# RWKV-7 steps on one core: PSUM banks shared out anew, first tokens in another order, new places for every piece, 16 projection pieces in each of the last steps

## The chip, the cores and the metric

The kernel runs on one core of a Trainium2 chip. What counts is the device time of one launch in microseconds (us). The kernel before was timed three times: 2500.08, 2500.66 and 2507.4 us, median 2500.66 us.

## What is computed

A decoder trunk of two layers over 2048 tokens of width 1024, all in float32. Layer 1 mixes tokens with gated linear attention (GLA), layer 2 with RWKV-7. Each layer is `x <- x + RMSNorm_post(mixer(RMSNorm_pre(x)))`. The RWKV-7 mixer, cut to what matters here:

```python
p = h @ w_in                          # 4224 columns: r, k, v, gate, decay rank 64, iclr rank 64
p = p + mu * (token_shift(p) - p)
decay = exp(-exp(w_log));  a = sigmoid(a0 + ad @ w_iclr_up)
def step(S, inp):                     # one token, 16 heads, S is 64 x 64 a head
    r_t, w_t, k_t, v_t, kk_t, a_t = inp
    sa = einsum('bhvk,bhk->bhv', S, -kk_t)
    S = S * w_t[:, :, None, :] + sa[..., None] * (kk_t * a_t)[:, :, None, :] + v_t[..., None] * k_t[:, :, None, :]
    y = einsum('bhvk,bhk->bhv', S, r_t)
    return S, y
y = groupnorm(y) * ln_w + ln_b + bonus
y = y * silu(gate);  return y @ w_out
```

## The kernel before, in words

**Stages.** The GLA layer comes first, with its output projection to about 911 us. Then RWKV runs in 32 steps (4 blocks of 512 tokens times 8 pairs of heads), and after the steps the rest of the output projection (`outproj`). A matrix product in nearly full precision is three products of split operands: `mm3` (L114) multiplies the high parts, high by low, and low by high. The high and low part of a weight are made by `split`; in the RWKV stage POOL makes them at L990 (`wh<-ws`) and L994 (`wl<-ws,wh`) in part of the pieces.

**One step.** `step` (L1144) works on 8 chunks of 64 tokens for two heads. Its pieces on TensorE (PE) are named by functions: `pA` the decayed products of keys and receptances (four pieces; mask L1370 on VectorE (DVE) takes them out of PSUM), `pL`, `pM`, `pW`, `pT` small 32x32 products that build the inverse of a triangular matrix, `pB` transposes, `pv` the values (two pieces; ScalarE (ACT) copies them out at L1325, `ve`), `pX` the product with the inverse `Ti` (ACT L1544 copies it to `Z`), `turn` transposes (ACT L1568), `pG` products whose results DVE adds to `BK` and `A` at L1583 (`G`), `pS` the chain of 8 states (ACT L1604, `next_state`, the last one L1604 into `S`), `py` the outputs (ACT L1618, `y_copy`), and `pg` the group norm's sums, which needs `y_sq` (L1623), `y_high` (L1628) and `y_low` (DVE L1633) of the outputs of the step before.

**Filler.** Between those pieces stand `f` pieces: a sixteenth of the projection work that the next step needs, 6 matmuls 128x512 each (`ps_pj<-R,wh` and `ps_pj<-R,wl`), called a chunk below. A step has 16 of them (12 in one early step, 20 in each eighth step by `MORE`). After the last step `END` gives how many still run in each further step: 12, with every fourth name of the sixteen left out.

**The order of the work.** Around the change the order is written out by hand: `put` (L86) gives each piece the time step number + `PLACE[name]`, `run` (L95) calls the pieces in that order under a manual schedule of PE, DVE, ACT and POOL. So the table `PLACE` sets the order on all four queues at once. A piece of step n with a place of 2.05 runs during step n+2; a step's work is spread over three to four steps.

**PSUM.** Eight banks, by the table `PB` (L70): `pj` 2 (projections), `tp` 2 (most of the step), `x` 1, `ch` 2 (states `pS` and `pg`), `y` 1. A new tile of a tag waits until the reader of the tile that had its bank is done.

```python
PB = dict(pj=2, tp=2, x=1, ch=2, y=1)
T.pv = self.ps("tp", [P, NC_ // 2, 2, C])
T.pA[cg] = [self.ps("tp", [P, 4, 2 * C]) for _ in range(2)]
T.pG[cg] = [self.ps("tp", [P, 4, 2 * C]) for _ in range(2)]
T.pS[c] = self.ps("ch", [P, 2, C])
```

**The start.** `start` (L566) orders the first four blocks of 128 tokens by hand: `square(j)` (ACT L328, waits for the tokens' DMA), `scale(j)` (POOL L308, DVE L337), `turn(j, k)` (PE transposes L343, ACT copy L345), weight splits `W0`, `W1`, `W2` (ACT L163, POOL L164), and `values(n)`, n pieces of the values' projection.

Of the kernel before, what the change touches and what calls it, by code (L numbers as in the profile page):

```python
# [50 lines left out]
class Trunk:  # L51
# [1035 lines left out]
    END = (12, 12, 12, 12)
    PLACE = _places(
        ("G", (2.044193, 2.050266, 2.091647, 2.158500)), ("Ti", (1.943141, 1.843493, 1.792896, 1.843393)),
        ("Tl", (1.896995, 1.931904)), ("X", (1.565836, 1.565936, 1.799057, 1.860390)), ("Z", (2.011437, 2.021714)),  # L1090
        ("a_exp", 0.211357), ("a_inv", 0.235809), ("a_ln", 0.212886), ("ae", (0.264280, 0.264380)),
        ("alpha", (1.784826, 1.830405, 1.928084, 1.927784)), ("bk_b", (0.393193, 0.393293)), ("bk_copy", 0.491543),
        ("bk_k", 0.393093), ("bonus", 0.827316), ("diag", (0.630464, 0.666138, 0.714265, 0.692811)),
        ("e", (1.976686, 0.550686, 0.225756, 0.383364)), ("e_minus", 0.227189), ("e_plus", 0.301397),
        ("elim", (0.804391, 0.807537, 0.807637, 0.871330, 0.906435, 0.906535, 0.906635, 0.906735, 0.937961, 0.960696,
          1.011273, 1.015145, 1.034379, 1.077861, 1.100228, 1.103822, 1.103922, 1.104449, 1.104549, 1.127910,
          1.134421, 1.135126, 1.136468, 1.158139, 1.187233, 1.196122, 1.210237, 1.248533)),
        ("ends", 0.408256), ("eye", (1.693688, 1.735073, 1.968882, 1.940955)),
        ("f", (0.255319, 0.000000, 0.050514, 0.774971, 0.318264, 0.976958, 0.509575, 0.349895, 0.478398, 0.529148,
          0.559227, 0.085857, 0.815059, 0.191123, 0.714834, 1.258740)),  # L1100
# [606 lines left out]
```

## Time and profile before

| what | before |
|---|---|
| median of the runs | 2500.66 us |
| the profiled execution, its own time | 2500.48 us |
| its span, first to last instruction | 2498.4 us |
| PE busy | 2404.0 us (96%) |
| ACT busy | 1646.3 us (66%) |
| DVE busy | 1601.1 us (64%) |
| POOL busy | 1065.7 us (43%) |
| mean granted clock of TensorE | 0.991 |

The span is what the profile covers; 2.1 us of the execution lie around it. Busy shares are means over stages with different limits. PE is nearly always busy, so the time is PE's work plus the stretches in which PE waits, and a piece that only changes its place costs or saves what it does to those waits.

### The profile page before, as it was taken

The page shows a single profiled execution, that of the slowest core. Times are in us where ns is not written, and L with a number is a line of the kernel's source. Part 1 is how long each engine was busy: PE and PEld are TensorE (multiplying, and loading weights), DVE is VectorE, ACT ScalarE, POOL GpSimd, SP SyncE. Part 2 cuts the span into 40 slices and gives each one's busy share as a digit, 9 for nine tenths or more (in the row PEclk, how much of TensorE's full clock was granted, in tenths as well). Part 3 has the DMA queues.
Part 4 walks back from the last instruction along what each step waited for, and adds up shares of the span by engine and source line. Part 5 has one row for each costly group of instructions (what it writes and reads, how often), then busy time and mean ns, then how long its engine had stood idle before and what let it go on. Part 6 is the DMA issues. An engine that isn't in the chain of part 4 may idle for free.

```text
span 2498.4 us, 53047 instructions
## 1 busy us (share of the span) xinstructions
PE 2404.0 (96%) x20049; PEld 2011.4 (81%) x20049; DVE 1601.1 (64%) x3339; ACT 1646.3 (66%) x3890; POOL 1065.7 (43%) x1557
## 2 busy tenths in 40 slices
PE   7999999999999998989999999999999999998998
PEld 6988888898878877767878788778788777887777
DVE  6544676346743368887777776777767787776432
ACT  6534565434533356876888988888888889886531
POOL 3213423123456556766543434334343434343442
PEclk9999999999999999998999999999999999999999
DMA  4211333113546565444433333333333333323482
GB/s 148 81 57 51 110 114 104 43 60 95 165 149 223 162 221 176 145 141 138 150 113 132 125 118 114 109 120 125 124 110 114 113 123 123 120 88 111 149 256 93
DMA packets 251863, 312.85 MB, mean 125 GB/s; under 512 B 18746, under 2 KB 180185, under 8 KB 251609
## 3 DMA queue, kind: packets, MB, share of 16 engines
q1 hardware_dynamic: 251608, 309.47, 37.4%
q8 instruction: 159, 2.61, 0.4%
q14 instruction: 96, 0.78, 0.1%
HBM read 230.77 MB, written 78.64 MB: 124 GB/s over the span
## 4 chain that ended last, share of the span: by engine, by line
PE 37%; ACT 18%; DVE 4%; issue 2%; DMA 1%; POOL 1%; POOLq 0%; SPq 0%; ACTq 0%; DVEq 0%
PE ps_pj L103 20%; PE ps_tp L103 9%; PE ps_x L103 3%; ACT AD L1380 2%; PE ps_ch L103 2%; ACT ve L1604 2%; ACT ts L836 1%; ACT ve L1325 1%; PE ps_y L103 1%; ACT BK L1397 1%; ACT y L1618 1%; PE ps_tp L1564 1%; ACT wt L1495 1%; ACT sq L1278 1%; DVE pp L1422 1%
## 5 line engine op out<-in xcount | busy, mean ns | idle before, releaser
L103 PE MATMUL ps_pj<-R,wh 128*128 128x512 f32 x3648 | 1172.8, 402 | 3.8 <-ACT wh L139 1.0
L103 PEld LDWEIGHTS ps_pj<-R,wh 128*128 128x128 f32 x3648 | 656.5, 190 | 131.0 <-issue 3.4
L103 PE MATMUL ps_pj<-R,wl 128*128 128x512 f32 x1824 | 718.2, 394 | 1.1 <-POOL wl L994 1.1
L103 PEld LDWEIGHTS ps_pj<-R,wl 128*128 128x128 f32 x1824 | 343.8, 188 | 79.8 <-POOL wl L994 1.9
L1604 ACT ACTIVATE ve<-ps_ch,cs 64x64 f32<-64x64 f32 x448 | 137.8, 308 | 61.3 <-PE ps_ch L103 52.5
L1422 DVE TENSOR_TENSOR pp<-L 128x14 f32<-128x14 f32 (+6 forms) x448 | 168.1, 375 | 10.5
L103 PE MATMUL ps_tp<-R,wh 128*128 128x512 f32 x512 | 158.3, 390 | 2.1 <-DVE ts L400 1.7
L1425 DVE TENSOR_TENSOR L<-L,pp 128x14 f32<-128x14 f32 (+6 forms) x448 | 139.9, 312 | 12.2
L832 POOL TENSOR_SCALAR carr<-ts 128x1 f32<-128x1 f32 x132 | 34.2, 259 | 241.1 <-ACT ts L836 240.8
L1551 POOL TENSOR_SCALAR A<-ra 64x512 f32<-64x512 f32 x128 | 90.0, 703 | 103.4 <-PE ps_x L103 51.9
L308 POOL TENSOR_TENSOR s<-s,cc 128x1 f32<-128x1 f32 (+1 forms) x96 | 57.6, 602 | 150.7 <-DVE s L306 138.4
L103 PE MATMUL ps_ch<-ve,BK 128*128 128x128 f32 x512 | 109.5, 296 | 7.8 <-ACT ve L1604 7.5
L103 PEld LDWEIGHTS ps_tp<-R,wh 128*128 128x128 f32 x512 | 95.8, 188 | 22.8 <-issue 2.5
L103 PEld LDWEIGHTS ps_ch<-ve,BK 128*128 128x128 f32 x512 | 87.1, 189 | 30.9 <-ACT ve L1604 11.4
L1380 ACT COPY AD<-A 32x128 f32<-32x128 f32 x256 | 105.1, 411 | 10.2 <-DVE A L1370 7.2
L836 ACT ACTIVATE ts<-ps_pj,prm 128x512 f32<-128x512 f32 x132 | 91.4, 692 | 18.7 <-PE ps_pj L103 10.7
L1370 DVE TENSOR_TENSOR A<-ps_tp,mask 128x512 f32<-128x512 f32 x128 | 82.3, 683 | 32.6 <-PE ps_tp L103 32.6
L103 PE MATMUL ps_tp<-R,wl 128*128 128x512 f32 x256 | 99.7, 390 | 0.0
L1583 DVE TENSOR_TENSOR BK<-ps_tp,BK 128x256 f32<-128x256 f32 x128 | 53.7, 419 | 69.6 <-PE ps_tp L103 69.6
L103 PE MATMUL ps_pj<-wh,R 128*128 128x256 f32 (+1 forms) x500 | 94.7, 287 | 0.0
L103 PE MATMUL ps_ch<-wh,R 128*128 128x256 f32 (+1 forms) x500 | 94.3, 286 | 0.0
L798 POOL TENSOR_SCALAR y<-BK,cs 128x256 f32<-128x256 f32 x64 | 36.6, 571 | 132.4 <-DVE BK L800 121.3
(358 smaller groups left out, 5518.3 us busy)
## 6 DMA issues: line engine op xcount, KB each, us to landing
wh<-w SPq DMA_DIRECT2D x99, 512.0 KB
wl<-w SPq DMA_DIRECT2D x99, 512.0 KB
w<-wh SPq DMA_DIRECT2D x33, 512.0 KB
w<-wl SPq DMA_DIRECT2D x33, 512.0 KB
Ti<-in_gla_w_in_dram SPq DMA_DIRECT2D x32, 512.0 KB
ws<-in_gla_w_in_dram SPq DMA_DIRECT2D x32, 512.0 KB
ws<-in_rwkv_w_in_dram SPq DMA_DIRECT2D x28, 512.0 KB
A<-in_x_dram SPq DMA_DIRECT2D x16, 512.0 KB
```

What stands on the lines that cost most here:

```text
L103: return self.nc.tensor.matmul(out, lhsT, rhs, start=start, stop=stop)
L308: nc.gpsimd.tensor_tensor(r[:, 0:w], u[:, 0:w], self.nhalf.broadcast_to([P, w]), op=ALU.pow)
L798: nc.gpsimd.tensor_scalar(Qf[:, n % 2, :], Qn, f[:, n:n + 1], 0.0, op0=ALU.mult, op1=ALU.add)
L832: self.put(name + ".carry", lambda: nc.gpsimd.tensor_scalar(cr, ts[:, TB:TB + 1], 1.0, 0.0, op0=ALU.mult, op1=ALU.add))
L836: nc.scalar.activation(ts[:, 1:TB + 1], pp, AF.Copy, scale=self.v["mu"][:, blk:blk + 1])
L1370: dve.tensor_mul(T.A[cg][:, :, :, h, :], V(T.pA[cg][h]), V(self.mask.unsqueeze(1).broadcast_to([P, 4, 2 * C])))
L1380: act.copy(T.AD[q, :, :, cg * 4:cg * 4 + 4].rearrange("p t u c -> p c u t"), T.A[cg][q, :, 0, h, 32 * b:32 * b + 32].rearrange("p c (u t) ...
L1422: dve.tensor_mul(T.u, T.M[:, s + 1:16, s:s + 1].broadcast_to([P, m, s]), T.M[:, s:s + 1, 0:s].broadcast_to([P, m, s]))
L1425: dve.tensor_add(T.M[:, s + 1:16, 0:s], T.M[:, s + 1:16, 0:s], T.u)
L1551: pool.tensor_scalar(T.A[cg][H[h], :, :, h, :], T.ra[H[h], cg * 4:cg * 4 + 4, :].rearrange("p c (b t) -> p c b t", b=2), 1.0, 0.0, op0=ALU ...
L1583: dve.tensor_add(o, T.pG[cg][h][:, :, x], o)
L1604: act.activation(o, x, AF.Copy, scale=k)
```

## The change

It does four things.

1. **Banks.** `ch` has one bank and a new tag `tv` has one. The values of `pv`, and the first tile of each pair that `pA` and `pG` write, take `tv`; the second tile of a pair stays in `tp`, which keeps two banks. In the GLA stage, which used both `ch` banks for values and for the transposes at the end of the output projection, the second use takes `tv`.
2. **Start.** `square(1)` and `scale(1)` stand behind the splits `W0` and ahead of `W1`; one piece of values stands ahead of `turn(1, .)`, two behind `square(2)`.
3. **End.** `END` is 16 in place of 12, in each of the four last steps.
4. **Places.** Every number of `PLACE` is new.

```diff
-    PB = dict(pj=2, tp=2, x=1, ch=2, y=1)
+    PB = dict(pj=2, tp=2, x=1, ch=1, tv=1, y=1)
...
-                tp = self.ps("ch", [P, 4, P])
+                tp = self.ps(("ch", "tv")[ch], [P, 4, P])
...
             square(0)
             scale(0)
-            square(1)
             turn(0, 0)
             W0[0]()
             turn(0, 1)
             W0[1]()
             W0[2]()
+            square(1)
+            scale(1)
             for part in W1:
                 part()
-            scale(1)
+            values(1)
             turn(1, 0)
             turn(1, 1)
             square(2)
-            values(3)
+            values(2)
             scale(2)
...
-            pv = [self.ps(t, [P, w]) for t in ("ch", "ch", "pj", "pj")]
+            pv = [self.ps(t, [P, w]) for t in ("ch", "tv", "pj", "pj")]
...
-    END = (12, 12, 12, 12)
+    END = (16, 16, 16, 16)
     PLACE = _places(
-        ("G", (2.044193, 2.050266, 2.091647, 2.158500)), ("Ti", (1.943141, 1.843493, 1.792896, 1.843393)),
+        ("G", (2.057791, 2.058873, 2.254885, 2.254985)), ("Ti", (1.929397, 1.883744, 1.720077, 1.821047)),
...
-                T.pv = self.ps("tp", [P, NC_ // 2, 2, C])
+                T.pv = self.ps("tv", [P, NC_ // 2, 2, C])
...
-                T.pA[cg] = [self.ps("tp", [P, 4, 2 * C]) for _ in range(2)]
+                T.pA[cg] = [self.ps(t, [P, 4, 2 * C]) for t in ("tv", "tp")]
...
-                T.pG[cg] = [self.ps("tp", [P, 4, 2 * C]) for _ in range(2)]
+                T.pG[cg] = [self.ps(t, [P, 4, 2 * C]) for t in ("tv", "tp")]
```

What the table moves is seen in PE's queue. The first place is in the middle of a step, on PE, from the first to the second piece of values (`ps_tp<-cen,vx` before, `ps_tv<-cen,vx` now) and on to the first product with `Ti`. Before:

```order
L103 MATMUL ps_tp_17338<-s_17258,bo 128x512
L103 MATMUL ps_tp_17354<-cen,vx_16513 128x128 x2
L103 MATMUL ps_pj_17279<-R_9711,wh_17104 128x512
...
L103 MATMUL ps_x_17374<-wt_17345,TT_17203 32x32 x16
L103 MATMUL ps_tp_17354<-cen,vx_16513 128x128 x2
L103 MATMUL ps_pj_17279<-R_9711,wh_17104 128x512
...
L103 MATMUL ps_tp_17447<-xw_13746,uh 128x512
L103 MATMUL ps_tp_17447<-xw_13746,ul_9162 128x512
L103 MATMUL ps_x_17451<-sq_17156,Ti_9165 128x128 x4
```

And now, at the same place:

```order
L103 MATMUL ps_tv_17321<-cen,vx_16500 128x128 x2
L103 MATMUL ps_pj_17276<-R_9719,wh_17092 128x512
...
L103 MATMUL ps_tp_17354<-kkx_17207,bo 128x512
L103 MATMUL ps_tp_17354<-s_17277,bo 128x512
L103 MATMUL ps_x_17357<-wt_17337,TT_17189 32x32 x16
L103 MATMUL ps_tv_17321<-cen,vx_16500 128x128 x2
L103 MATMUL ps_pj_17276<-R_9719,wh_17092 128x512
...
L103 MATMUL ps_x_17420<-sq_17193,Ti_9165 128x128 x4
```

Before, one chunk and `pT` (`ps_x<-wt,TT`) stood between the two pieces of values, now two chunks, the sums `pb` (`ps_tp<-kkx,bo` and `s,bo`) and `pT`. Before, two chunks and `pw` (`ps_tp<-xw`) stood between the second piece and the product with `Ti`, now one chunk.

The second place is later in the same step, on PE: the two pairs of `pG`, `<-sq,A` and `<-a,A`. Before:

```order
L103 MATMUL ps_tp_17486<-sq_17156,A_16542 128x128
L103 MATMUL ps_tp_17487<-sq_17156,A_16542 128x128
...
L103 MATMUL ps_pj_17444<-R_9711,wh_17275 128x512
...
L103 MATMUL ps_tp_17507<-a_17348,A_16543 128x128
L103 MATMUL ps_tp_17508<-a_17348,A_16543 128x128
```

And now:

```order
L103 MATMUL ps_tv_17467<-sq_17193,A_16552 128x128
L103 MATMUL ps_tp_17468<-sq_17193,A_16552 128x128
...
L103 MATMUL ps_x_17478<-a_17344,Ti_9165 128x128 x4
L103 MATMUL ps_pj_17460<-R_9719,wh_17272 128x512
...
L103 MATMUL ps_tp_17498<-xa_13767,uh 128x512
L103 MATMUL ps_tp_17498<-xa_13767,ul_9162 128x512
L103 MATMUL ps_ch_17507<-ve_16786,BK_16750 128x128
L103 MATMUL ps_tv_17516<-a_17344,A_16553 128x128
L103 MATMUL ps_tp_17517<-a_17344,A_16553 128x128
```

Between the pairs stood one chunk (six matmuls); now the second `pX`, a chunk, `pa` (`ps_tp<-xa`) and the first state stand there.

The third place is the end of a step, on PE: from the second piece of outputs (`ps_y<-A,ve`) to the group norm's sums (`ps_ch<-sq,bo` and `a,bo`) that are made of them. Before:

```order
L103 MATMUL ps_ch_17661<-ve_16781,BK_16735 128x128
L103 MATMUL ps_y_17670<-A_16543,ve_16781 128x128 x4
L103 MATMUL ps_pj_17598<-R_9711,wh_17440 128x512
...
L103 MATMUL ps_tp_17720<-ra_17657,bk_17663 128x128
L103 MATMUL ps_tp_17721<-ra_17657,bk_17663 128x128
...
L103 MATMUL ps_ch_17730<-sq_17679,bo 128x512
L103 MATMUL ps_ch_17730<-a_17706,bo 128x512
```

And now:

```order
L103 MATMUL ps_pj_17576<-R_9719,wl_17457 128x512
L103 MATMUL ps_y_17683<-A_16553,ve_16787 128x128 x4
L103 MATMUL ps_pj_17682<-R_9719,wh_17572 128x512
...
L103 MATMUL ps_ch_17717<-sq_17699,bo 128x512
L103 MATMUL ps_ch_17717<-a_17710,bo 128x512
...
L103 MATMUL ps_tv_17730<-ra_17647,bk_17657 128x128
L103 MATMUL ps_tp_17731<-ra_17647,bk_17657 128x128
...
L103 MATMUL ps_x_17742<-TD_17720,A_17142 32x32 x16
...
L103 MATMUL ps_tv_17782<-ra_17647,bk_17657 128x128
```

Before, three chunks and the first pair of `pA` (`<-ra,bk`) stood between the outputs and the sums; now two chunks. Both pairs of `pA` come after the sums, with `pL` alone (`ps_x<-TD,A`) between them, and ahead of the outputs stands a chunk in place of a state.

## Rows read from the trace of the kernel before

**Rows 1.** The page: busy time of the engines

```profile
PE 2404.0 (96%) x20049; PEld 2011.4 (81%) x20049; DVE 1601.1 (64%) x3339; ACT 1646.3 (66%) x3890; POOL 1065.7 (43%) x1557
```

**Rows 2.** Busy time by stretch: PE, PEld, DVE, ACT, POOL, granted clock, DMA share, GB/s

```profile
911.00:1185.00 274.00, 247.75 (x2353) 199.41 (x2352) 219.24 (x404) 199.09 (x465) 183.56 (x227) 0.96 0.45 151
1185.00:2245.00 1060.00, 1033.05 (x11027) 844.49 (x11026) 787.54 (x1759) 902.74 (x2136) 446.98 (x805) 1.00 0.34 119
2245.00:2345.00 100.00, 89.81 (x902) 73.17 (x901) 53.99 (x126) 70.79 (x172) 45.84 (x54) 0.97 0.37 118
```

**Rows 3.** A group of PE, 1290 to 2245 us: busy, mean ns, idle before and its releaser

```profile
L103 PE MATMUL ps_tp<-cen,vx 128*128 128x128 f32 x184 | 30.9, 290 | 17.9 <-ACT ve L1325 16.3 <-ACT BK L1397 1.2
```

**Rows 4.** Timeline of PE from step to step: start, length, engine, line, operation, idle before

```profile
1454.75 0.50 PE L103 MATMUL ps_ch<-sq,bo 128*128 128x512 f32 x1
...
1490.87 1.16 PE L103 MATMUL ps_y<-A,ve 128*128 128x128 f32 x8 [0.24 <-ACT y L1618]
1491.78 0.71 PE L103 MATMUL ps_pj<-R,wh 128*128 128x512 f32 x2
...
1497.16 0.50 PE L103 MATMUL ps_ch<-sq,bo 128*128 128x512 f32 x1
...
1510.15 0.71 PE L103 MATMUL ps_tp<-cen,vx 128*128 128x128 f32 x4 [0.83 <-ACT ve L1325]
1510.62 0.71 PE L103 MATMUL ps_pj<-R,wh 128*128 128x512 f32 x2
...
1513.45 0.40 PE L103 MATMUL ps_tp<-xw,uh 128*128 128x512 f32 x1
...
1516.74 1.16 PE L103 MATMUL ps_tp<-sq,A 64*128 64x128 f32 x16
...
1539.16 0.50 PE L103 MATMUL ps_ch<-sq,bo 128*128 128x512 f32 x1
```

**Rows 5.** Timeline of ACT in the same step

```profile
1497.70 0.41 ACT L1527 COPY sq<-BK 64x256 f32<-64x256 f32 x1 [2.35 <-PE ps_ch L103]
...
1509.03 1.08 ACT L1325 COPY ve<-ps_tp 64x128 f32<-64x128 f32 x4
...
1511.92 0.74 ACT L1516 COPY Ti<-ps_x 32x256 f32<-32x256 f32 x2
```

**Rows 6.** Timeline of DVE in the step of rows 4

```profile
1494.03 0.69 DVE L1633 TENSOR_TENSOR a<-ce,sq 128x512 fp32r<-128x512 f32 x1 [1.06 <-ACT ce L1623]
...
1497.26 1.29 DVE L1370 TENSOR_TENSOR A<-ps_tp,mask 128x512 f32<-128x512 f32 x2 [0.46 <-PE ps_tp L103]
```

**Rows 7.** Waits of PE, 911 to 1290 us: total, times, longest

```profile
PE ps_tp L103 <- DVE A L1583: 8.5, 4, 2.9
```

**Rows 8.** Timeline of PE around one such wait

```profile
1123.84 2.71 PE L103 MATMUL ps_tp<-a,A 64*128 64x128 f32 x16 [2.87 <-DVE A L1583]
```

**Rows 9.** Timeline of DVE ahead of it

```profile
1119.28 2.46 DVE L1425 TENSOR_TENSOR L<-L,pp 128x50 f32<-128x50 f32 x1
...
1122.02 0.22 DVE L1425 TENSOR_TENSOR L<-L,pp 128x54 f32<-128x54 f32 x1
```

**Rows 10.** Timeline of POOL ahead of it

```profile
1119.27 2.40 POOL L994 TENSOR_TENSOR wl<-ws,wh 128x1024 fp32r<-128x1024 f32 x1
```

**Rows 11.** Waits of PE, 2245 to 2346 us

```profile
PE ps_ch L103 <- ACT ve L1604: 4.8, 6, 1.1
PE ps_tp L103 <- DVE A L1583: 2.2, 1, 2.2
```

**Rows 12.** Timeline of PE in one of the last steps

```profile
2300.67 0.49 PE L103 MATMUL ps_ch<-ve,BK 128*128 128x128 f32 x2 [1.11 <-ACT ve L1604]
```

**Rows 13.** Timeline of ACT at the start

```profile
8.89 1.06 ACT L328 ACTIVATE R<-A 128x1024 fp32r<-128x1024 f32 x1 [3.37 <-DMA A<-in_x_dram]
```

**Rows 14.** Timelines of POOL and of PE at the start, one row of each

```profile
10.95 2.74 POOL L164 TENSOR_TENSOR ra<-Ti,ra 128x272 fp32r<-128x272 f32 x3
...
15.12 2.16 PE L103 MATMUL ps_ch<-ra,R 128*128 128x272 f32 x8
```

More of the change, by code (lines that the diff above doesn't have):

```diff
@@ L1085, in rwkv @@
             pass
[L1087 removed]
+    END = (16, 16, 16, 16)
     PLACE = _places(
[L1089 to L1108 removed]
[5 rows of a table removed]
[L1114 to L1127 removed]
@@ new lines @@
+        ("e", (0.915143, 0.495091, 0.004495, 0.312517)), ("e_minus", 0.191565), ("e_plus", 0.263047),
+        ("elim", (0.868681, 0.868781, 0.871196, 0.919666, 0.933614, 0.952142, 0.955207, 0.955307, 0.986238, 0.997043,
+          0.999399, 1.001229, 1.065811, 1.075616, 1.198678, 1.203157, 1.203257, 1.216976, 1.217076, 1.236678,
+          1.254947, 1.278886, 1.285049, 1.285149, 1.285192, 1.333255, 1.382271, 1.401332)),
+        ("ends", 0.479514), ("eye", (2.040937, 1.839415, 2.066864, 2.037152)),
@@ new lines @@
+        ("kx.high", 0.111167), ("kx.low", 0.000000), ("kx.mu", 0.034267), ("kx.sum", 0.029304), ("lanes", 0.731905),
+        ("low", 0.000000), ("low16", 1.648917), ("mask", (0.583854, 0.665698, 0.668432, 0.675897)),
+        ("n_exp", 0.316493), ("n_ln", 0.291725),
+        ("next_state", (2.106521, 2.186252, 2.255661, 2.271972, 2.293186, 2.359124, 2.443100, 3.028979)),
+        ("out.high", 0.069957), ("out.low", 0.064583), ("pA", (0.583654, 0.583754, 0.640310, 0.661127)),
[5 rows of a table added]
+        ("py", (2.285831, 2.484813)), ("r_high", 0.651447), ("r_low", 0.710870), ("r_mul", 0.528444),
@@ new lines @@
+        ("ra_a", 0.364273), ("ra_r", 0.402070), ("rx.carry", 0.000000), ("rx.high", 0.030431), ("rx.low", 0.098494),
+        ("rx.mu", 0.051553), ("rx.sum", 0.000000), ("s_exp", 0.000000), ("s_inv", 0.034824), ("s_ln", 0.022155),
+        ("scan", 0.118487), ("sg.carry", 0.044015), ("sg.high", 0.196236), ("sg.low", 0.000000), ("sg.mu", 0.029164),
+        ("sg.sum", 0.121349), ("sg_exp", 2.698384), ("sg_inv", 2.938921), ("sg_ln", 2.714790), ("sg_mul", 2.940456),
+        ("spread", (1.485457, 1.512426, 1.512526, 1.517589)), ("state", 1.382171), ("swap", 0.058982),
@@ new lines @@
+        ("tanh1", 0.003213), ("tanh2", 0.170327), ("tanh3", 0.007827), ("tanh4", 0.133594),
+        ("tokens", (0.789636, 0.817519)), ("turn", (2.004669, 2.012633)), ("turned", (2.013256, 2.014701)),
+        ("unit", 0.322667), ("unit_diag", 1.333155), ("up", (0.648137, 0.698798, 0.980181)),
+        ("ve", (0.842861, 1.008529)), ("vx.carry", 0.001457), ("vx.high", 0.078141), ("vx.low", 0.069351),
+        ("vx.mu", 0.116796), ("vx.sum", 0.079648), ("wa.carry", 0.003483), ("wa.high", 0.709989),
@@ L1128 @@
+        ("wa.low", 0.879892), ("wa.mu", 0.076285), ("wa.sum", 0.020004), ("wt", (1.780001, 1.787818)),
+        ("y_bonus", 2.707933), ("y_copy", (2.383638, 2.498877)), ("y_gate", 3.073780), ("y_high", 2.506883),
+        ("y_low", 2.516923), ("y_norm", 2.624351), ("y_sq", 2.504460), ("zero", 0.000000),
     )
```

31 lines of the change are left out of this document (9 added, 22 removed), and 10 rows, old and new, of the table PLACE.

## The prediction

> **What bounds the kernel.** I read the page first: PE is busy for 2404.0 us of the 2498.4 us span [rows 1], so a change that leaves PE's work alone can win at most the 94 us in which PE stands still. The order of the change shows the same number of instructions on PE, so this is one of waits. Busy time by stretch tells where they lie [rows 2]: 26.3 us (274.00 - 247.75) in the first RWKV steps, 27.0 us (1060.00 - 1033.05) in the steady ones, 10.2 us (100.00 - 89.81) in the last ones. The granted clock there is 0.96, 1.00 and 0.97, so the first and last steps also lose time to the clock. A group of PE and its timeline name the waits of the steady steps: the second piece of values, with 17.9 us of idle in 23 steps, 0.78 each [rows 3], and in the step shown 0.83, and the outputs with 0.24 [rows 4]. ACT says why: the copies L1325 that free the values' tile begin at 1509.03 in a queue that has run without a marked gap since 1497.70, when `pg` released it [rows 5]. So ACT, let go once a step by `pg`, is the second limit.
>
> **Steady steps, some 25 of them.** A step takes 42.2 us: two lie between the `pg` at 1454.75 and that at 1539.16 [rows 4]. Measure from the `pg` between them, at 1497.16. `ve` ends at 1509.03 + 1.08 = 1510.11 [rows 5], 12.95 us later. PE asked for its tile at 1510.15 - 0.83 = 1509.32 [rows 4], after 12.16. From `pg` to that piece the new order has the same pieces and four chunks, and the first pair of `pA` besides, which has come behind `pg`: 1.1 us, as the pair of `pG` of the same size [rows 4]. PE comes after 13.3 us, and the 0.83 shrinks to 0, or to 0.6 in steps where a copy of the next block (ACT L180) falls into the burst. But behind that piece stands one chunk, where two and `pw` stood. A piece of values takes 0.47 (1510.15 to 1510.62) and a chunk 1.41 (two lie between 1510.62 and 1513.45, all [rows 4]), so PE is at `pX` after 13.3 + 1.9 = 15.2, while the last `Ti` copies end at 1511.92 + 0.74 = 1512.66 [rows 5], after 15.5. With the hand-over and the slips, I take 0.4 to 1.05 us for both waits together, 0.7 in the middle.
>
> The outputs' 0.24 goes, since a chunk now stands ahead. Two new waits come. Between the pairs of `pA` only `pL` is left, and both want the one bank `tv`; a mask takes 0.65 us (1.29 for two [rows 6]), and `pL` is a piece of about that length, so I put 0.1 to 0.2. And `pg` stands two chunks, 2.8 us, behind the outputs, while what it needs takes 2.9: the outputs end at 1491.78, where the next chunk starts [rows 4], and DVE L1633 ends at 1494.03 + 0.69 = 1494.72 [rows 6]. Before, `pg` came 2.4 us after that. Here too 0.1 to 0.2. Sum per step: -0.83 - 0.24 + 0.7 + 0.15 + 0.15, near zero. Against it stands that the new queue breaks its chunks into 12 runs a step where there were 13, and that the gaps too short to be marked shrink with the waits; a walk through the whole new step with the lengths of the trace's rows gives 41.3 to 42.0 us. I take -0.25 us a step, between the two: **-6 us**. Bounds: every idle microsecond of the stretch gone, -27 [rows 2]; 0.6 us more a step, +15.
>
> **First steps.** Four waits of the second pair of `pG` for DVE's additions cost 8.5 us [rows 7], one more in the last steps 2.2 [rows 11]. At 1123.84 it is 2.87 us [rows 8]: DVE's L1425 took 2.46 us beside POOL's L994 of 2.40, against 0.22 for a like one just after [rows 9, 10], and the additions were late. The change puts the second `pX`, `pa` and a state beside the one chunk between the pairs, some 1.7 us more, and sends first tiles to another bank. Taking 1.6 from each of five waits is **-8 us**; bounds 0 and -10.7. The clock: after that idle `pG` took 2.71 us, against 1.16 in a steady step [rows 4, 8], so PE ran at its lower level. A mean of 0.96 over 274 us [rows 2] is at most 11 us of lost work. Three of the falls follow such waits, and with shorter waits I expect one or two to go: **-4 us**, bounds 0 and -11.
>
> The lateness is a collision of POOL with DVE. The Trainium skill, SBUF - State Buffer, "Who interferes with whom", calls the port pair that the two share an exclusive lock; 2.46 us beside 2.40 agrees with it. By that rule the new order, which keeps every one of these splits, keeps the late additions too; that is rival C.
>
> **Last steps.** 16 chunks, 16 x 1.41 = 22.6 us of the output projection, move from behind the steps into them; PE's work is the same. Before, states stand there in pairs without a chunk between, and the second waits for ACT, as at 2300.67 with 1.11 us [rows 12]; six such waits cost 4.8 us [rows 11]. Idle there is 10.2 us [rows 2], of which 2.2 is counted above. I take 4.5 us of the rest and 1.5 of the clock (0.97 of 100 us is 3 at most): **-6 us**, bounds -11 and +3, should the pieces' weights, split on POOL, come late.
>
> **Start.** ACT's copies for the first `turn` stood behind `square(1)`, which waited 3.37 us for its tokens and ran from 8.89 for 1.06 [rows 13]; the first product of values came at 15.12, though POOL had its split ready at 10.95 + 2.74 = 13.69 [rows 14]. Up to 1.4 us are to be had, but the next tokens are later: **-0.5 us**, bounds 0 and -1.5.
>
> **One bank for states** costs nothing while chunks stand between states, as they mostly do; the first state of a step must now wait until ACT has read the last one of the step before, which the new places put ahead of it in ACT's queue. If that cover is gone, it is the 0.8 to 1.1 us of one such pair [rows 11, 12]. The Trainium skill, PSUM - Partial Sum Buffer, "Summary: rules for kernel authors", advises to write a different bank than the one being read while matmuls run; that speaks against one bank for a chain of states, and no run here shows it yet. The GLA stage writes the same products to a bank of another name: 0.
>
> **Sum.** -6 - 8 - 4 - 6 - 0.5 = -24.5 us against the profiled execution's 2500.48, which stands 0.2 below the median of the runs: **2476 us**.
>
> **The rivals.**
> A. ACT's queue sets the step, and the wait only moves from the second piece of values to the first `pX`, to `pG` and to `pg`. For it: ACT's gapless run of 11 us, and `Ti` 15.5 us after `pg`. Against it: ACT is idle for 157 of the 1060 us [rows 2]. Steady gain 0: 2500.48 - 18.5 = 2482.
> B. Slower: `pg` follows too close on the outputs. If `y_copy` stands behind other work in ACT's queue, the chain of 2.9 us grows, `pg` slips, and with it ACT's whole burst and all that waits for it. Before, 2.4 us of spare covered this; now nothing does. With 1.2 us a step it is +30 in place of -6: 2500.48 + 30 - 18.5 = 2512. It decides from (18.5 + 7.5) / 25 = 1.04 us a step. For it: the cover of 2.8 against 2.9. Against it: ACT idled 2.35 us before `pg` released it [rows 5], so its queue is empty there.
> C. Splits on POOL hold DVE as before, so the first steps' -8 and -4 don't come: 2500.48 - 12.5 = 2488. For it: the 2.46 us beside 2.40 [rows 9, 10]. Against it: the 1.7 us of cover hold for whatever makes the additions late.
> A and C together leave -6.5: 2494. That the change doesn't do what it says is excluded by the order.
>
> **How the numbers follow.** About 0.3%, 7.5 us, is what a measurement of this kernel can tell from no change; so faster is below 2493. My forecast gets 0.42, A 0.15, C 0.11: faster 0.68. A and C together, 0.14, and the mild half of B, 0.05: the same, 0.19. The rest of B: slower, 0.13. The range reaches from 2456, where most marked waits of the steady steps go besides (-20 more), to 2506, short of B's price.
>
> **What would show it.** Right: the group of the values' products has under 0.5 us of idle a step; the second pair of `pG` waits under 3 us in all before 1290; the first RWKV steps show a clock above 0.96; no `ps_ch` waits of 0.7 us and more in the last steps. Rival A: idle before `ps_x<-sq,Ti`, by ACT, of 0.7 us a step. Rival B: idle before `ps_ch<-sq,bo`, released by DVE L1634 or ACT, of over 0.5 us a step. C: another L1425 of some 2.4 us beside L994 with a `pG` wait behind it. I am wrong if steady steps get longer, or if the last steps' idle does not shrink.

## The result, and the profile after

The changed kernel takes 2440.61 us (median of 4 runs, 2436.86 to 2443.27) against 2504.03 us of the kernel before in the same comparison: a ratio of 0.9759, 95% interval 0.9738 to 0.9779. It is 2.4% faster, some 60 us (60.1 between the two profiled spans, 63.4 between these medians) where 24 were forecast, and lies below the range of 2456 to 2506. Medians, here and below, are of the runs in the usual state, without the few executions that took far longer than the rest of their kernel.

The profiled execution took 2440.03 us, its span is 2438.3 us. PE's busy time fell though its instructions are the same, and with it DVE's; against [rows 1] the page now has:

```profile
PE 2374.7 (97%) x20049; PEld 1995.5 (82%) x20049; DVE 1535.5 (63%) x3339; ACT 1650.8 (68%) x3890; POOL 1062.4 (44%) x1557
```

The same stretches as in [rows 2], busy time by engine, granted clock, DMA share, GB/s:

```profile
911.00:1185.00 274.00, 260.03 (x2690) 211.72 (x2690) 227.87 (x440) 221.67 (x516) 204.61 (x249) 0.99 0.50 168
1185.00:2245.00 1060.00, 1044.83 (x11216) 861.99 (x11215) 740.78 (x1812) 926.58 (x2183) 449.50 (x818) 1.00 0.35 121
2245.00:2345.00 100.00, 94.97 (x647) 76.45 (x646) 51.86 (x86) 54.27 (x130) 46.39 (x43) 1.00 0.54 175
```

The idle time of PE in the first stretch fell from 26.3 to 14.0 us and the clock rose from 0.96 to 0.99. Since the work inside a window of fixed times has moved, `pg`, which comes once a step, is the better mark. The timeline of PE in the kernel before, at the first `pg`, the eighth and the 29th:

```profile
1006.09 0.49 PE L103 MATMUL ps_ch<-sq,bo 128*128 128x512 f32 x1
...
1327.48 0.50 PE L103 MATMUL ps_ch<-sq,bo 128*128 128x512 f32 x1
...
2228.30 0.50 PE L103 MATMUL ps_ch<-sq,bo 128*128 128x512 f32 x1
```

And in the changed kernel:

```profile
1002.51 0.50 PE L103 MATMUL ps_ch<-sq,bo 128*128 128x512 f32 x1 [0.93 <-ACT sq L1629]
...
1299.57 0.40 PE L103 MATMUL ps_ch<-sq,bo 128*128 128x512 f32 x1
...
2177.28 0.40 PE L103 MATMUL ps_ch<-sq,bo 128*128 128x512 f32 x1
```

| stretch | before | after | difference | forecast |
|---|---|---|---|---|
| start to the first `pg` | 1006.1 | 1002.5 | -3.6 | -0.5 and a little of the first steps |
| first `pg` to the eighth | 321.4 | 297.1 | -24.3 | -10.4 (four of the five waits, and the clock), and 7 steps' share of the steady gain |
| eighth to the 29th, 21 steps | 900.8 | 877.7 | -23.1 (1.1 a step) | -0.25 a step |
| 29th to the end of the span | 270.1 | 261.0 | -9.1 | -6, and 1.6 of a wait of `pG` |

Two terms were far too small: the steady steps and the first steps. In the steady steps an ordinary step takes 41.1 us (1464.23 to 1505.35 from `pg` to `pg`) where it took 42.2. The busy time in the 21 steps from the eighth `pg` to the 29th, in the columns of [rows 2], was before

```profile
1327.50:2228.30 900.80, 877.14 (x9341) 717.91 (x9339) 667.51 (x1500) 769.10 (x1818) 364.94 (x676) 1.00 0.33 119
```

and is now

```profile
1299.60:2177.30 877.70, 865.14 (x9340) 714.33 (x9338) 609.25 (x1502) 772.65 (x1819) 358.99 (x676) 1.00 0.35 122
```

PE's idle time fell from 23.7 to 12.6 us, 0.53 a step, and its busy time by 12.0 us, 0.57 a step, with the same instructions and a clock of 1.00 in both. So half of the gain in these steps lies neither in idle time nor in the clock. (The profile models the ends of matmuls; how much of its busy time is work it does not show.) The groups of PE in the steady part, 1262 to 2177 us, with idle before and its releaser, answer to [rows 3]:

```profile
L103 PE MATMUL ps_y<-A,ve 128*128 128x128 f32 x352 | 46.3, 275 | 0.0
L103 PE MATMUL ps_tv<-cen,vx 128*128 128x128 f32 x176 | 31.3, 300 | 1.6 <-ACT ve L1326 1.6
...
L103 PE MATMUL ps_tv<-sq,A 64*128 64x128 f32 x176 | 25.4, 285 | 4.9 <-ACT A L1569 4.9
...
L103 PE MATMUL ps_x<-sq,Ti 128*128 128x128 f32 x176 | 24.7, 283 | 4.6 <-POOL A L1552 4.6
```

The wait of the values fell from 17.9 us to 1.6 and that of the outputs is gone. The two waits that came, for the first `pG` and the first `pX`, are 0.2 us a step each.

One step on PE, against [rows 4]:

```profile
1464.23 0.40 PE L103 MATMUL ps_ch<-sq,bo 128*128 128x512 f32 x1
...
1476.87 0.69 PE L103 MATMUL ps_x<-wt,TT 32*32 32x32 f32 x32
1477.49 0.71 PE L103 MATMUL ps_tv<-cen,vx 128*128 128x128 f32 x4
...
1479.80 1.13 PE L103 MATMUL ps_x<-sq,Ti 128*128 128x128 f32 x8 [0.20 <-POOL A L1552]
```

And on ACT, against [rows 5]:

```profile
1464.97 0.69 ACT L1643 ACTIVATE ce<-ps_ch,cc 128x512 f32<-128x512 f32 x1
...
1476.29 1.08 ACT L1326 COPY ve<-ps_tv 64x128 f32<-64x128 f32 x4
...
1479.29 0.40 ACT L1502 COPY Ti<-TD 32x256 f32<-32x256 f32 x1
```

`ve` ends at 1477.37, 13.14 us after `pg`: ACT is no earlier than before (12.95). PE is later: it comes to the second piece of values after 13.26 and finds the bank free. It comes to `pX` after 15.4, at 1479.60, when the last `Ti` copy ends at 1479.69, after 15.46. The two engines now arrive together. The row names POOL L1552 for this wait of 0.20 us:

```profile
1478.24 1.32 POOL L1552 TENSOR_SCALAR A<-ra 64x512 f32<-64x512 f32 x2 [1.63 <-issue]
```

It ended at 1479.56, before PE came, so of the two it is the `Ti` copy that came last.

In the first steps no wait for DVE's additions L1584 is left. The longest waits of PE from 911 to 1265 us are these, where [rows 7] had 8.5 us for the additions:

```profile
PE ps_pj L103 <- POOL wl L995: 2.7, 2, 1.8
PE ps_x L103 <- issue: 2.5, 3, 2.0
PE ps_ch L103 <- ACT ve L1605: 1.7, 2, 1.0
```

### The profile page after: what moved, and what is told of

It reads as the page before. It is cut to its first block, busy times and chain, and to the rows that moved or that the text cites. A ratio compares the mean times of both kernels' runs of the same rounds, so it can differ in the third digit from the quotient of the medians.

```text
span 2438.3 us, 52892 instructions
## 1 busy us (share of the span) xinstructions
PE 2374.7 (97%) x20049; PEld 1995.5 (82%) x20049; DVE 1535.5 (63%) x3339; ACT 1650.8 (68%) x3890; POOL 1062.4 (44%) x1557
## 5 line engine op out<-in xcount | busy, mean ns | idle before, releaser
L1426 DVE TENSOR_TENSOR L<-L,pp 128x14 f32<-128x14 f32 (+6 forms) x448 | 134.6, 301 | 8.1
L1423 DVE TENSOR_TENSOR pp<-L 128x14 f32<-128x14 f32 (+6 forms) x448 | 129.2, 288 | 11.0
L1552 POOL TENSOR_SCALAR A<-ra 64x512 f32<-64x512 f32 x128 | 80.8, 631 | 55.4 <-issue 34.2
L1584 DVE TENSOR_TENSOR BK<-ps_tv,BK 128x256 f32<-128x256 f32 x64 | 26.9, 421 | 117.2 <-PE ps_tp L103 117.1
L995 POOL TENSOR_TENSOR wl<-ws,wh 128x1024 fp32r<-128x1024 f32 x36 | 87.4, 2429 | 1.8
L139 ACT CAST wh<-ws 128x512 fp32r<-128x512 f32 (+2 forms) x74 | 40.9, 602 | 68.7 <-PE ps_pj L103 68.6
```

The source lines that it names most:

```text
L139: self.nc.scalar.copy(hi[:, c], src[:, c])
L995: nc.gpsimd.tensor_sub(lo, st, hi.bitcast(F32))
L1423: dve.tensor_mul(T.u, T.M[:, s + 1:16, s:s + 1].broadcast_to([P, m, s]), T.M[:, s:s + 1, 0:s].broadcast_to([P, m, s]))
L1426: dve.tensor_add(T.M[:, s + 1:16, 0:s], T.M[:, s + 1:16, 0:s], T.u)
L1552: pool.tensor_scalar(T.A[cg][H[h], :, :, h, :], T.ra[H[h], cg * 4:cg * 4 + 4, :].rearrange("p c (b t) -> p c b t", b=2), 1.0, 0.0, op0=ALU ...
```

## The experiments

Each label is one kernel. In the edits of `PLACE` only the entries that change are shown. Times are medians, with the ratio to the kernel before and its 95% interval.

**e1_banks_only.** The banks without the places.

```diff
-    PB = dict(pj=2, tp=2, x=1, ch=2, y=1)
+    PB = dict(pj=2, tp=2, x=1, ch=1, tv=1, y=1)
```

and the five lines that take `tv`, as in the change; the rest is the kernel before.

> The kernel before with the new share-out of PSUM banks alone (old places, old start, END 12). Theory 'places': the gain of the steady steps comes from where the new order puts PE against ACT's queue, the banks only permit that order; then a steady step stays at 42.0 to 42.6 us, the second piece of values still waits some 0.8 us for ACT's copies L1325, and the time stays within 8 us of the kernel before (2492 to 2512), rather slower, because pairs of states now share one bank. Rival 'banks': values and pairs of products in a bank of their own are what frees PE; then a steady step falls to 41.2 to 41.6 us and the time to 2470 to 2480.

Measured: 2501.81 us, 0.9998 (0.9988 to 1.0007). Steps take 42.3 us, and the values' wait is there, as the waits of PE from 911 to 2245 us show:

```profile
PE ps_tv L103 <- ACT ve L1325: 19.4, 22, 1.3
...
PE ps_ch L103 <- ACT S L1604: 6.3, 4, 1.8
```

The banks alone give nothing. One bank for the states does bring waits with the old places, four in which the first state waits for ACT to read the last one of the step before (6.3 us); in the sum they can't be told. In the changed kernel they are not there.

**e2_pa_ahead.** The changed kernel with one pair put back ahead of `pg`.

```diff
-("pA", (0.583654, 0.583754, 0.640310, 0.661127))
+("pA", (0.543000, 0.543100, 0.640310, 0.661127))
```

> The changed kernel with the first pair of pA back ahead of pg, where it stood before; nothing else moves. Theory 'places': PE then comes to the second piece of values 1.1 us earlier after pg, while ACT's copies are not earlier; its wait comes back with 0.7 to 1.0 us a step, a steady step takes 41.9 to 42.2 us instead of 41.17, and the time is 2460 to 2468. Rival 'banks': no change beyond 5 us of the changed kernel's 2440, for the banks are the same.

Measured: 2474.99 us, 0.989 (0.9875 to 0.9905): 34 us of the 60 are lost again. A step takes 42.4 us. The timeline of PE in one of them:

```profile
1445.48 0.71 PE L103 MATMUL ps_tv<-cen,vx 128*128 128x128 f32 x4 [1.10 <-ACT ve L1326]
```

The wait came back as the theory said, and larger: 1.1 us, since `pA` is 1.1 us of work and PE had been at ACT's heels. The time is above the expected 2460 to 2468, as the wait costs 1.2 us a step, not 0.7 to 1.0.

**e3_end12.** The changed kernel with the old `END`.

```diff
-    END = (16, 16, 16, 16)
+    END = (12, 12, 12, 12)
```

> The changed kernel with END 12 as before. Theory 'END': the 16 chunks in the last steps are what covers the waits of states there, so the last stretch (from the pg at about 2177 us on) gets 5 to 9 us longer and the time is 2446 to 2450. Rival 'places in the tail': the new places alone cover the states; then the time is 2438 to 2443.

Measured: 2441.82 us, 0.9753 (0.9738 to 0.9767), which can't be told from the changed kernel. Theory 'END' missed. The waits it spoke of do come back; the waits of PE from 2194 to 2300 us have, with END 12,

```profile
PE ps_ch L103 <- ACT ve L1605: 4.4, 5, 1.1
```

and with 16, in the changed kernel,

```profile
PE ps_ch L103 <- ACT ve L1605: 0.8, 1, 0.8
```

but of these 3.6 us only 2.7 are seen at the end of the profiled spans (2441.0 and 2438.3) and 1.2 in the medians.

**e4_pg_close.** The changed kernel with less cover between the pairs of `pG`.

```diff
-("G", (2.057791, 2.058873, 2.254885, 2.254985))
+("G", (2.054000, 2.054100, 2.254885, 2.254985))
-("Z", (1.981484, 2.064862))
+("Z", (1.981484, 2.055300))
-("pG", (2.014501, 2.014601, 2.089520, 2.108113))
+("pG", (2.014501, 2.014601, 2.055500, 2.055600))
```

> The changed kernel with the second pair of pG directly behind the second pX and its chunk, ahead of pa and the first state, and with DVE's additions of the first pair called a little earlier; the cover between the pairs shrinks by some 0.8 us a step. Theory 'cover': in the first RWKV steps the waits of the second pair for DVE's additions come back, 3 to 8 us in all, and a fall of the clock with them; steady steps change by less than 0.1 us; time 2443 to 2452. Rival 'the collisions are gone': in the new order no L1425 beside L994 falls ahead of the additions, so nothing waits there and the time stays at 2438 to 2443.

Measured: 2474.69 us, 0.9886 (0.9869 to 0.9902). Both theories missed, since the edit did more than was meant: it took the pair out from between the first two states, and the second state now waits for ACT in each step. Waits of PE from 911 to 2245 us:

```profile
PE ps_ch L103 <- ACT ve L1605: 23.3, 32, 1.0
...
PE ps_tv L103 <- DVE A L1584: 2.5, 2, 1.7
```

A step takes 42.17 us, 1.0 more. So the second pair of `pG` is itself the cover of the state chain in the new order. Of the waits for the additions two came back, 2.5 us.

**e5_pa_behind_only.** The kernel before, old banks, with two numbers changed.

```diff
-("pA", (0.531789, 0.544892, 0.587574, 0.606821))
+("pA", (0.555000, 0.555100, 0.587574, 0.606821))
```

> The kernel before, old banks, old start, END 12, with two numbers of the old table changed: the first pair of pA stands directly behind pg instead of ahead of it. Theory 'PE late for the values': this alone takes away the wait of the second piece of values (0.8 us), so a steady step takes 41.3 to 41.8 us instead of 42.4 and the time is 2474 to 2486. Rival 'ACT's queue': the wait only moves on to the first pX or to a state, steps stay above 42.1, time 2493 to 2502; then banks and the rest of the places are needed too.

Measured: 2478.33 us, 0.9909 (0.9891 to 0.9927): 22.5 us from moving one pair of products behind `pg`. Steps take 41.2 to 41.7 us; the values' wait does not stand among the longest any more. The waits of the first steps stayed, here from 911 to 1290 us:

```profile
PE ps_tp L103 <- DVE A L1583: 7.2, 4, 2.9
```

**e6_pg_cover.** The changed kernel with one chunk and one state between the pairs of `pG`, and the pair still between the states.

```diff
-("pX", (1.980924, 2.017199))
+("pX", (1.980924, 2.014300))
-("pa", 0.055942)
+("pa", 0.136000)
```

> The changed kernel with the second pX ahead of the first pair of pG and pa behind the second state, so that between the pairs of pG stand one chunk and one state, as much as in the kernel before (one chunk); the second pair stays between the first two states. Theory 'cover': in steady steps nothing changes by more than 0.2 us, but in the first steps the waits of the second pair for DVE's additions return, with 3 to 8 us in all before 1290 us, and falls of the clock behind them with up to 7 us; time 2445 to 2456. Rival 'no collision falls there any more': no such waits, time 2436 to 2445.

Measured: 2447.45 us, 0.9781 (0.9766 to 0.9797), 6.8 us above the changed kernel, near the low end of what theory 'cover' gave. Steps take 41.3 us, 0.2 more. In the first steps two waits came, not four, and at a state instead of the second pair:

```profile
PE ps_ch L103 <- DVE BK L1584: 3.8, 2, 2.4
```

Less cover costs something, but not what the first steps had gained. That left a question: had the additions themselves become less late?

**e7_px_after_pw.** An attempt at a faster version.

```diff
-("pX", (1.980924, 2.017199))
+("pX", (2.000500, 2.017199))
-("Z", (1.981484, 2.064862))
+("Z", (2.000600, 2.064862))
-("s_exp", 0.000000)
+("s_exp", 0.014900)
```

> An attempt at a faster version: the changed kernel with pw ahead of the first pX, and ACT's s_exp behind the copies of the transposes. It should cover the wait of the first pX for POOL's alpha (0.2 us in 22 steps) and that of the first pG for ACT's copies L1569 (0.27 us in 29 steps): up to 0.5 us a step, 12 us in all, if nothing else is late there: 2428 to 2438. If ACT's queue sets these times, the waits move behind and the time stays at 2437 to 2444.

Measured: 2465.7 us, 0.9856 (0.9843 to 0.987), 25 us slower than the changed kernel. A step takes 42.06 us. The longest waits of PE from 911 to 2245 us:

```profile
PE ps_tp L1565 <- ACT A L1569: 11.6, 18, 0.7
PE ps_tp L103 <- ACT A L1569: 9.7, 30, 0.6
```

`pw` holds one of the two `tp` banks until `s_exp` has read it; with `s_exp` late the transposes wait for each other's bank.

**e8_f_in_pa.** The changed kernel with the chunk behind `pg` moved between the pairs of `pA` (`f10`).

```diff
-("f", (... 0.577397, 0.202052, ...))
+("f", (... 0.630000, 0.202052, ...))
```

> The changed kernel with the chunk behind pg moved in between the pairs of pA, behind pL. Theory: pL takes 0.17 us more a step in the changed kernel, because the second pair waits for the mask of the first in the one bank tv; with a chunk between them that goes: 3 to 5 us less, 2435 to 2438. Rival: the first pair then stands directly behind pg and waits for its own operands (ACT L1302 or POOL), and the time stays or rises by up to 5 us.

Measured: 2452.34 us, 0.9803 (0.979 to 0.9816), 12 us slower. Without the chunk ahead of it, 1.4 us of work, PE comes to `pL` before DVE's transpose L1444 is there; waits from 911 to 2245 us:

```profile
PE ps_x L103 <- DVE TD L1444: 24.2, 29, 1.5
```

Behind `pg` the chunk had covered the wait for this transpose, and that was worth more than covering the mask.

**e9_pa_pg_old_banks.** The kernel of e5 with the second pair of `pG` moved back as well.

```diff
-("G", (2.044193, 2.050266, 2.091647, 2.158500))
+("G", (2.044193, 2.050266, 2.154200, 2.158500))
-("pG", (2.042512, 2.043850, 2.078154, 2.078254))
+("pG", (2.042512, 2.043850, 2.154000, 2.154100))
```

> The kernel before with old banks, old start and END 12; beside the first pair of pA behind pg (2478 by itself) the second pair of pG goes behind the first state and one more chunk, so that two chunks and a state, some 3.1 us, lie between the pairs instead of one chunk, 1.6. Theory 'cover': the 7 to 8 us of waits for DVE's additions (L1583) before 1290 us go, and with them falls of the clock: the pg of the eighth step comes 8 to 18 us earlier than in the run with pA alone, time 2460 to 2471. Rival 'collisions elsewhere': the late additions now hold up a state or the next product instead, 2473 to 2480.

Measured: 2581.21 us, 1.0328 (1.0306 to 1.0349), some 80 us slower than the kernel before. Waits of PE from 911 to 2245 us:

```profile
PE ps_tp L103 <- DVE L L1425: 68.3, 28, 3.8
```

and in a steady step the timeline of PE shows where:

```profile
1511.97 0.47 PE L103 MATMUL ps_tp<-xa,uh 128*128 128x512 f32 x1 [2.47 <-DVE L L1425]
```

With all of this in two `tp` banks, `pa` behind the pair needs a bank that the pair holds, and DVE reads that bank only behind its eliminations: the additions L1583 that free it end at 1511.82, beside the elimination that the row names. Neither theory had that. These places do not fit two `tp` banks. They are not the places of the change, where `pa` stands ahead of the second pair, so that those need `tv` is not shown by it.

**e10_oldstart.** The changed kernel with the old order in `start`.

```diff
             scale(0)
+            square(1)
             turn(0, 0)
...
-            square(1)
-            scale(1)
             for part in W1:
                 part()
-            values(1)
+            scale(1)
             turn(1, 0)
             turn(1, 1)
             square(2)
-            values(2)
+            values(3)
```

> The changed kernel with the old order of the first tokens. Theory: the new start is worth 0 to 1.5 us, so 2440 to 2443 and no difference that can be told. Rival: the 3.6 us by which the changed kernel's first pg came earlier are the start's, then 2443 to 2445.

Measured: 2437.57 us, 0.975 (0.9734 to 0.9766). The intervals overlap: the start is worth nothing that can be told.

**e11_pw_late.** Another attempt at a faster version of the changed kernel.

```diff
-("pw", 0.000000)
+("pw", 0.014800)
-("s_exp", 0.000000)
+("s_exp", 0.014900)
```

> An attempt at a faster version: the changed kernel with pw behind the first pair of pG, and ACT's s_exp behind the copies L1569 of the transposes. Theory: the copy that the first pG waits for (0.27 us in 28 steps) comes 0.7 us earlier while PE comes 0.5 us earlier, so the wait shrinks by 0.1 to 0.2 us a step: 2435 to 2439. Rival: the chain from s_exp to the scan gets late, or pw's bank is missed, and the time is 2441 to 2455.

Measured: 2484.39 us, 0.9933 (0.9919 to 0.9947), 44 us slower. The waits of PE from 911 to 2245 us are headed by

```profile
PE ps_tv L103 <- ACT a L1545: 38.4, 28, 1.5
```

The second pair of `pG` waits for ACT's copy of the second `pX`, which comes late behind `pw` on PE and `s_exp` on ACT.

**e12_end16_only.** The kernel before with the new `END` alone.

```diff
-    END = (12, 12, 12, 12)
+    END = (16, 16, 16, 16)
```

> The kernel before with END 16 alone. The prediction's term for the last steps: chunks between the states there take away 4 to 6 us of waits and clock, 2492 to 2497. Rival, after the run with END 12 in the changed kernel showed nothing: the waits move, the last outputs come later by the chunks' time, and the time stays within 3 us of the kernel before.

Measured: 2499.46 us, 0.9997 (0.9985 to 1.001). The states' waits for ACT behind 2245 us do fall, from 4.8 us [rows 11] to 0.8, but the time stays: the moved chunks give nothing by themselves that can be told, and at most 4 us by the interval.

**e13_g_first.** The kernel before with five eliminations and the gate called behind the additions; on DVE alone.

```diff
-("elim", (... 0.937961, 0.960696, 1.011273, 1.015145, 1.034379, 1.077861, ...))
+("elim", (... 1.051000, 1.051050, 1.051100, 1.051200, 1.051300, 1.077861, ...))
-("y_gate", 3.027929)
+("y_gate", 3.051400)
```

> The kernel before (old banks, start, END 12) with five elimination pieces of DVE (L1422, L1425) and the gate L1675 called behind the additions L1583 of the first pair of pG instead of ahead of them; PE's order is the old one. Theory 'order on DVE': in three of the first steps those pieces, which read two operands from SBUF, are held for 2.4 us by POOL's L994 and the additions queue behind them; with the additions first, which ran at 0.41 us beside L994 in the changed kernel, the waits of the second pair of pG before 1290 us (7.9 us) fall under 2 and the clock's falls go with them: 8 to 16 us less, 2485 to 2493, steady steps within 0.3 us. Rival 'cover on PE': the additions themselves are late or too long for one chunk, waits stay above 5 us, 2496 to 2503.

Measured: 2493.76 us, 0.9964 (0.995 to 0.9979), 8.6 us less, at the low end of the gain that theory 'order on DVE' gave (8 to 16), and a time 0.8 us above its range. The waits for the additions from 911 to 1290 us fell from 8.5 us [rows 7] to

```profile
PE ps_tp L103 <- DVE A L1583: 1.9, 4, 0.6
...
PE ps_ch L103 <- DVE BK L1583: 0.7, 1, 0.7
```

and the first stretch of [rows 2] now has a clock of 0.98 in place of 0.96:

```profile
911.00:1185.00 274.00, 251.83 (x2408) 202.58 (x2407) 218.09 (x414) 205.57 (x480) 186.41 (x236) 0.98 0.46 156
```

PE's order is the old one, with one chunk between the pairs, so these waits go without more cover on PE.

**e14_g_first_pa.** The edits of e5 and e13 together, in the kernel before.

```diff
-("elim", (... 0.937961, 0.960696, 1.011273, 1.015145, 1.034379, 1.077861, ...))
+("elim", (... 1.051000, 1.051050, 1.051100, 1.051200, 1.051300, 1.077861, ...))
-("pA", (0.531789, 0.544892, 0.587574, 0.606821))
+("pA", (0.555000, 0.555100, 0.587574, 0.606821))
-("y_gate", 3.027929)
+("y_gate", 3.051400)
```

> Both found parts in the kernel before: additions first on DVE, and the first pair of pA behind pg. If the two are what the change gains, they add up: 22 for pA and 8 to 16 for the additions, 2462 to 2471. If the eliminations, now later, are then late for pL, steady steps get longer and it is 2475 or more.

Measured: 2471.84 us, 0.9878 (0.9863 to 0.9893), 30.5 us less; 22.5 and 8.6 make 31.1, so the two parts add up. Half of the change's gain is had with the old banks, the old start and the old end. One wait comes with it: `pg` now waits for DVE L1633 in four of the first steps, as it does in e5 (3.9 us). The waits of PE from 911 to 2245 us have

```profile
PE ps_ch L103 <- DVE a L1633: 4.3, 4, 1.5
```

where the changed kernel has a single one of 0.2. The busy time in the 21 steps from the eighth `pg` on is

```profile
1319.20:2204.10 884.90, 876.54 (x9339) 718.64 (x9339) 651.91 (x1501) 770.03 (x1818) 351.49 (x677) 1.00 0.34 121
```

**e15_elim_first.** The changed kernel with two eliminations and the gate put ahead of the additions.

```diff
-("elim", (... 1.001229, 1.065811, 1.075616, 1.198678, ...))
+("elim", (... 1.001229, 1.057000, 1.057100, 1.198678, ...))
-("y_gate", 3.073780)
+("y_gate", 3.057200)
```

> The changed kernel with two elimination pieces and the gate L1676 ahead of the additions of the first pair of pG, as the kernel before had such pieces there. Theory 'order on DVE': in the first steps POOL's L995 holds them and with them the additions, pG or a state waits again with 3 to 7 us in all before 1290 us, 2444 to 2456. Rival 'cover on PE': the 3 us of cover hide it, 2437 to 2443.

Measured: 2445.67 us, 0.9773 (0.9758 to 0.9788), 5 us slower, as theory 'order on DVE' said. The intervals of the two ratios overlap, but the runs do not (2444.92 to 2447.04 against 2436.86 to 2443.27), and the trace from the first `pg` to the eighth is 8.3 us longer. The timeline of DVE in the fourth step shows the collision again:

```profile
1149.71 2.46 DVE L1423 TENSOR_TENSOR pp<-L 128x54 f32<-128x54 f32 x1
1152.20 0.22 DVE L1426 TENSOR_TENSOR L<-L,pp 128x54 f32<-128x54 f32 x1
...
1152.84 0.74 DVE L1676 SCALAR_TENSOR_TENSOR sg<-y,prm,sg 128x512 f32<-128x512 f32 x1
1153.51 0.41 DVE L1584 TENSOR_TENSOR BK<-ps_tv,BK 128x256 f32<-128x256 f32 x1
```

POOL at that time, and PE behind it:

```profile
1149.70 2.40 POOL L995 TENSOR_TENSOR wl<-ws,wh 128x1024 fp32r<-128x1024 f32 x1
```

```profile
1154.73 0.77 PE L103 MATMUL ps_ch<-ve,BK 128*128 128x128 f32 x2 [2.13 <-DVE BK L1584]
```

In the changed kernel a split stands beside the additions, and holds only the elimination behind them. DVE there, in the third step:

```profile
1109.05 0.42 DVE L1584 TENSOR_TENSOR BK<-ps_tv,BK 128x256 f32<-128x256 f32 x1 [3.05 <-PE ps_tp L103]
...
1110.05 0.41 DVE L1584 TENSOR_TENSOR A<-ps_tp,A 128x256 f32<-128x256 f32 x1
1110.38 1.27 DVE L1423 TENSOR_TENSOR pp<-L 128x56 f32<-128x56 f32 x1
```

and POOL:

```profile
1109.17 2.41 POOL L995 TENSOR_TENSOR wl<-ws,wh 128x1024 fp32r<-128x1024 f32 x1
```

## Why the prediction was wrong, and where it was right

**What bounds the kernel: right for the waits, not for all of the gain.** The values' wait behind ACT was the largest of the steady steps, as said. But the prediction let the change win at most the time in which PE stands still, and what the clock costs. Of the 60.1 us between the spans, 30.8 are PE's idle time (94.4 to 63.6) and 29.3 its busy time. By the mean clock, 0.991 and now 0.997, some 14 of these 29 are the clock's, which is an estimate. The other 15, of which 12 lie in the 21 steady steps, had no term of their own, only the words on gaps too short to be marked.

**Steady steps: the mechanism right, the size wrong.** The failed step is the sum "-0.83 - 0.24 + 0.7 + 0.15 + 0.15, near zero", and the -0.25 made of it. About half of the miss is in its waits, mostly in the 0.7, and half in the time outside the marked waits, for which the -0.25 left 0.2 a step where the trace shows 0.57. I had PE at the second piece of values after 13.3 us and at `pX` after 15.2, against `Ti` after 15.5; the trace has 13.26, 15.4 and 15.46. The arithmetic held to 0.2 us, and its own answer for the two waits was 0 and 0.3. "With the hand-over and the slips" I made 0.4 to 1.05 of that; measured are 0.1 (1.6 us in 22 steps) and 0.2. The 0.15 for `pg` did not come: no wait of it is among those of the steady part, though the spare of 2.4 us is used up. The 0.15 for the mask came in full: `pL` to the next `pA` takes 0.17 us more. Missed was the 0.2 of the first `pG`. So the marked waits fell by some 0.5 us net, where I had next to none, and the step by 1.1 to 1.3: added up by kind of piece from start to start over two steps of each kernel, `pT` with the wait behind it gives 0.88, the states 0.46 (among them the last one, which stood with the outputs' wait behind it), and `pX` and `py` 0.15 each, while `pL` and the chunks take 0.26 back, and the transposes of `turn`, `pv`, `pw` and `pb` some 0.1 each. The walk that I quoted, 41.3 to 42.0, had the better answer, and I went to a value at its upper end (42.2 - 0.25). That PE's place against ACT is the cause of the values' wait is shown from both sides: e2 took the pair back (+34), e5 moved it alone (-22.5), while e1 gave nothing.

**First steps: the place right, the cause wrong.** The waits went, all four, and the clock rose to 0.99. In e13's trace, where the additions stand first and the rest is old, the stretch from the first `pg` to the eighth is 12.1 us shorter (309.3), about the 10.4 forecast for waits and clock; the other half of the 24.3 had no term but the steady steps'. But I gave the credit to 1.7 us of cover on PE. e13 leaves PE alone and takes 8.6 us; e15 puts two pieces back on DVE and loses 5 with all the cover there; e6 shows that cover has a part too, a few microseconds: of its 6.8 some 4 are the 0.2 a step of the steady part. Rival C failed at its core: it held that the splits, all kept, would hold DVE as before. They do run, 18 of them from the first `pg` to the eighth in either kernel, but what stands beside them has changed. The Trainium skill, SBUF - State Buffer, "Who interferes with whom", calls the shared port pair an exclusive lock, and has a DVE instruction with two inputs in SBUF contend with a GpSimd instruction that reads SBUF; the trace agrees (L1423 2.46 us beside L995 of 2.40). It does not follow that any DVE work is held: the additions, with one operand in PSUM, took 0.41 us beside an L995 of 2.41 in the changed kernel. I read the rule without asking which instruction stands there.

**Last steps: the size about right, the cause only in part.** The stretch got 9.1 us shorter, against 7.6 forecast. `END`, to which I put it, gives 1 us or nothing by the medians of e3 and e12, though the states' waits go with it; one of 0.8 us is left, where I had asked for none of 0.7. The traces divide the stretch from the 29th `pg` on. In the kernel before, e13 and e14 it takes 270.1, 270.6 and 268.8 us, and one wait of some 2 us for the additions, with a fall of the clock, stands in the last steps; in e1 and e5, with the same old `END`, neither stands there, and it takes 264.9 and 265.4. With the new `END` it takes 262.4 in e12 and 261.0 in the changed kernel, and 264.2 in e3 with the old one. So by single traces some 5 us hang on that wait and 3 on `END`. Why the wait comes in some of these kernels and not in others is not shown.

**Start and one bank: right.** e10 can't be told from the changed kernel, e1 not from the kernel before, though the wait of a step's first state that was feared does come there.

**The rivals.** A held in small part: most of the wait went, and 0.2 us a step each came at `pX` and at the first `pG`, both behind copies of ACT. B did not come: `pg` shows no wait in the steady part. The range failed because its lower end added 20 us to a middle that was too high by 35.

**What stays open.** e14 has 30.5 of the 60 us with the old banks. Against its profile the changed kernel is another 14 us faster from the first `pg` to the eighth, 7 in the next 21 steps (a third of a microsecond each), 8 behind them and 5 ahead of the first `pg`. Of the 14, the waits of `pg` for DVE, which e14 has and the changed kernel has not, are some 4. The 7 are not idle time: e14's PE stands still for 8.4 us there (884.90 - 876.54) and the changed kernel's for 12.6, but its busy time is 876.5 against 865.1. From start to start over these steps the states give 0.43 us a step, `py` 0.17 and `pX` 0.15, and other pieces take some back. Which of the new places does that, and why, is not shown. That the new banks are needed for it is not shown either: no run has the places of the change with the old banks. No version that was tried is faster than the changed kernel beyond the interval.

## What to carry to other kernels

Where two engines follow each other once a step, measure both from the event that releases them, and compare arrival with arrival: a product that was moved from ahead of that event to behind it made the waiting engine late enough, and the time fell (e5). When such a sum gives a small wait, forecast that wait, and put doubts into the range. Do not take the busy time of the bound engine as fixed because its instructions are: here a new order took 12 us of it in 21 steps, at full clock. Before crediting cover on the bound engine, look at what stands ahead of the late instruction on its own engine, and which of those pieces another engine can hold up; moving a few of them behind it cost nothing that could be told in e13 and e14.

## What was not expected of the hardware

POOL's split of 2.4 us held DVE instructions with both operands in SBUF for its whole length (2.46 us in place of 0.22), while additions and masks that read PSUM beside it ran at their usual 0.41 and 0.68 us (in the changed kernel masks of 0.67 and 0.69 us stand at 1089.35 and 1090.08 beside a split from 1088.65 to 1091.02). PE's busy time from the first `pg` to the eighth fell by 13 us, from 303.2 to 289.9, with the same instructions. The busy time by stretch has, before,

```profile
1006.10:1327.50 321.40, 303.21 (x3112) 246.42 (x3111) 249.78 (x506) 256.36 (x605) 191.27 (x262) 0.97 0.40 137
```

and after

```profile
1002.50:1299.60 297.10, 289.87 (x3111) 238.71 (x3111) 228.16 (x502) 257.79 (x606) 188.22 (x260) 0.99 0.44 148
```

So of the 24.3 us of this part 11 are PE's idle time (18.2 to 7.2) and 13 its busy time. Busy time times granted clock is some 294 us before and 287 after, so only 6 of the 13 are what PE's lower level cost behind the waits; the other 7, like the 12 of the steady steps, lie at full clock and stay unexplained. DVE's busy time fell by 21.6 us there as well. The eliminations L1422 and L1425 (L1423 and L1426 in the changed kernel), 196 in each with both operands in SBUF, have 11.4 of it (77.97 to 66.61); how much of the rest POOL's instructions had held was not separated.
